# Rewriting the first stage of a hybrid attention layer, up to the first transposed activations

## The chip, the cores and the metric

The kernel runs on one core of a Trainium2 chip. The core has five engines, each with an instruction queue of its own: TensorE (PE, matrix products), VectorE (DVE), ScalarE (ACT), GpSimd (POOL) and SyncE (SP, which here only issues transfers). Each works through its queue in order and waits where an input is not there yet. Transfers between DRAM and the on-chip memory (SBUF) are issued by SP, ACT or POOL and run on 16 DMA engines that all queues share. Products land in PSUM, of which one bank holds 128 x 512 f32.

The metric is the device time of one execution in microseconds (us), as a median of runs.

## The reference

One decoder layer over 2048 rows of 1024. A vector `c` gives a shift, a scale and a gate (adaLN); the rows are normalised, modulated, projected once for two kinds of attention, gated, projected back, normalised and added to the input.

```python
mod = jax.nn.silu(c) @ w_ada[l] + b_ada[l]
shift, scale, gate = jnp.split(mod, 3, axis=-1)
h = rms_norm(x, g_pre[l]) * (1.0 + scale[:, None, :]) + shift[:, None, :]
proj = h @ w_in[l]
qa, ka, va, fa, za, qb, kb, vb, zb = jnp.split(proj, split_points, axis=-1)
oa = forgetting_attention(qa, ka, va, fa + b_fgate[l])      # reshaped to heads
oa = oa * jax.nn.silu(za)
ob = sliding_window_sink_attention(rope(qb), rope(kb), vb, sinks[l])
ob = ob * jax.nn.silu(zb)
y = jnp.concatenate([oa, ob], axis=-1) @ w_out[l]
x = x + gate[:, None, :] * rms_norm(y, g_post[l])
```

What matters here is all that stands before the first product of `h` with a piece of `w_in`: `silu(c) @ w_ada` for shift and scale, the mean squares of the first rows of `x`, the rotary angles, and the preparation of the first weights.

## The kernel before

**Number format.** Large products run on f16 pairs. A f32 matrix is scaled by a power of two and split into a high f16 half and a low one (what is left); a product is then three f16 products (high-high, high-low, low-high). So each piece of weights needs the maximum of its absolute values first, and so does `h`: `pH` is a power of two below a bound on `h`, and `Gp` and `Shp` are gain and shift divided by it.

**h^T.** The 2048 rows are four chunks of 512 (`ci`); `hT[ci]` holds chunk `ci` transposed, for each of eight groups `k` of 128 columns a high and a low tile of 128 x 512. `turn(ci, k)` transposes four 128 x 128 blocks of normalised x on PE into one PSUM tile (five such tiles in rotation); `scaled` then writes the f32 tile `hf` (three in rotation) by ACT with gain and shift, for even `k` the high half too; `split` writes the high half by DVE for odd `k`, and the low half by DVE.

**The first stage** (lines 418 to 642) is written in one block of manual order: within such a block each engine executes in the order of the text. It loads rows, `w_ada` (eight blocks of 512 KB for the scale, `load_ada(1, k)`, eight for the shift, `load_ada(0, k)`), x rows 0 to 3 (`load_x`), the first weights `kb`, `vb`, `zb0` and x rows 4 to 7. `silu(c) @ w_ada` is done on PE with the vector repeated over 128 columns (`ada_pe`, f32 products) and partly on DVE (`ada_dve`: multiply and add into `acc`, summed over partitions by `ada_sum`). `ada_col` takes a result that lies in every partition back to one column per group by a product with the identity and a sum on DVE. `squares`, `root` and `normal` make the mean squares (ACT), their inverse roots (DVE) and the scaled rows. The bound on `h` is 32 times the gain plus the shift, its maximum taken over columns, by a transpose over partitions, and spread again by a product (lines 613 to 621). `spread` sends the rotary factors to their partitions.

**The second block** (from line 1042) runs the projections. Its work on PE is a list `punits` of units; for chunk 0 these are eight of `kb`, eight of `vb`, eight of `zb0`, eight of `zb1`, with `turn_x(1, k)` for the next chunk put in between (`at_`, line 948). Before unit `n` the functions in `events[n]` are written out, and after every second unit `tick` runs what earlier units left for later (evacuations). The two blocks are merged by a planner with estimated times, each block's own order on each engine being kept; so an instruction of the second block can come ahead of later ones of the first.

**A weight's way** (`add`, line 900): eight steps with leads in units ahead of its first product: `w_load` (POOL's queue, 512 KB), `w_max` (maximum per partition on DVE; POOL stores it to DRAM, `mx_d`), `w_back` (POOL loads it back, spread over all partitions, `mxr`), `w_scale` (maximum and power of two on DVE), `w_high` (ACT), `w_low` twice (DVE), `w_done`. For `zb0` maximum and spread are done on chip instead (`z_row` and `z_all`, lines 927 to 934, through PSUM bank 2). `evac_rope` (line 687) evacuates `kb` and `qb`: ACT copies, SP swaps halves by four transfers (`qs`), POOL multiplies by the sine (line 711), DVE adds (line 712), ACT and DVE split.

**The windows.** After `N_PRO - 4` units the sliding-window attention starts: `scores` (PE), `maxima` (DVE), `exps` (ACT), `turn` (PE) per window, with the remaining projection units in between.

## Time and profile before

| what | value |
|---|---|
| median of 3 runs | 1220.69 us (1217.82 to 1222.75) |
| profiled execution, device time | 1218.8 us |
| its span, first to last instruction | 1216.6 us |
| PE busy | 1158.6 us, 95% of the span |
| DVE, ACT, POOL busy | 74%, 55%, 12% |
| mean granted PE clock | 0.985 of full speed |
| moved by DMA | 120.71 MB |

The profile is of one execution. An instruction's row gives its start and length, engine, line of the kernel, operation, `output<-input`, shape, and in brackets the time its engine stood idle before it and what ended that. A row with `xN` merges N neighbours. A transfer's row on SP or POOL is its issue; its landing is seen by who waits for it. In a table of stretches the columns are the stretch, its length, busy time (and count) of PE, PE's weight loads, DVE, ACT and POOL, then the granted PE clock, the share of time the DMA engines were busy, and GB/s; where PE alone is asked for, only PE's column stands between length and clock.

### The profile page before, as it was taken

Reading aid. Unit: us, or ns where it says so; the run is one execution under the profiler, and the core shown is the slowest. Engines: PE = TensorE matmul, PEld = TensorE weight load, DVE = VectorE, ACT = ScalarE, POOL = GpSimd, SP = SyncE. Lnnn points to the kernel's source line nnn. Section 1 sums busy time; section 2 is a strip of 40 time slices with the busy share of each in tenths; the row PEclk is TensorE's granted clock in tenths of the full one; section 3 lists DMA queues with packets and bytes.
Section 4 is the critical chain, followed back from the end, with each engine's and each line's share of the span. In section 5 each row is a group of like instructions: output and inputs, shape, how many; then the busy total and the mean of one; then the engine's idle time right before and its main releaser. Section 6 shows DMA issues by size and latency. Waiting matters only on the chain.

```text
span 1216.6 us, 27400 instructions
## 1 busy us (share of the span) xinstructions
PE 1158.6 (95%) x10832; PEld 693.8 (57%) x10832; DVE 904.4 (74%) x2268; ACT 674.7 (55%) x1117; POOL 142.7 (12%) x252
## 2 busy tenths in 40 slices
PE   6599989999999999999999999999999979999997
PEld 2367657655568876555555555555555545555553
DVE  6676657677777647688888798878978797666665
ACT  2675435555555542566666666666766778333231
POOL 2001122233322211010010110010000000000000
PEclk8899999999999999999999999999999989999999
DMA  9645333334322322323334322122111135445652
GB/s 324 204 131 168 82 77 60 67 94 92 96 78 69 57 60 54 72 61 82 83 60 84 86 60 79 39 71 49 39 44 43 58 117 187 144 156 191 198 169 83
DMA packets 88036, 120.71 MB, mean 99 GB/s; under 512 B 27836, under 2 KB 63716, under 8 KB 87908
## 3 DMA queue, kind: packets, MB, share of 16 engines
q1 hardware_dynamic: 76932, 85.94, 24.3%
q0 software_dynamic: 10976, 33.03, 12.0%
q8 instruction: 85, 1.39, 0.6%
q14 instruction: 43, 0.35, 0.1%
HBM read 71.56 MB, written 25.18 MB: 80 GB/s over the span
## 4 chain that ended last, share of the span: by engine, by line
PE 82%; DVE 9%; DMA 5%; issue 2%; ACT 2%; SPq 1%; POOL 0%; DVEq 0%; ACTq 0%; POOLq 0%
PE bk L307 32%; PE bk L1406 13%; PE bk L325 6%; PE sta L1257 4%; PE bk L1208 4%; PE sta L1258 4%; PE poa L1283 2%; PE poa L1284 2%; PE poa L1281 2%; PE pxb L864 2%; PE bk L740 2%; DMA qs<-qf 2%; PE pss L831 2%; PE pob L883 2%; DVE pha L1271 1%
## 5 line engine op out<-in xcount | busy, mean ns | idle before, releaser
L1264 ACT ACTIVATE p<-sta,lift,scl_qk 128x1024 f32<-128x1024 f32 (+2 forms) x160 | 172.0, 1075 | 135.1 <-PE sta L1258 78.7
L307 PE MATMUL bk<-hT,wh_qk 128*128 128x512 f16 x768 | 194.7, 378 | 0.4 <-DVE a_m L1211 0.4
L1406 PE MATMUL bk<-wohl,oz 128*128 128x512 f16 x768 | 172.4, 379 | 1.9 <-ACT wohl L1346 0.8
L1271 DVE TENSOR_TENSOR pha<-p,pha 128x1024 f16<-128x1024 f32 (+2 forms) x160 | 169.1, 1057 | 0.0
L1211 DVE TENSOR_REDUCE a_m<-bk 128x1 f32<-128x512 f32 x192 | 130.2, 686 | 52.3 <-PE bk L1208 51.7
L1268 ACT ACTIVATE pha<-p 128x1024 f16<-128x1024 f32 (+2 forms) x160 | 148.0, 925 | 6.4 <-PE poa L1284 1.3
L1406 PEld LDWEIGHTS <-oz 128*128 128x128 f16 x768 | 74.4, 99 | 83.9 <-issue 1.8
L1281 PE MATMUL poa<-vt,pha 128*128 128x65 f16 x1088 | 117.4, 193 | 2.7 <-DVE ona L1290 2.7
L1284 PE MATMUL poa<-vt,pha 128*128 128x65 f16 x1088 | 117.1, 193 | 1.1 <-DVE pha L1271 1.1
L1283 PE MATMUL poa<-vt,pha 128*128 128x64 f16 x1088 | 117.4, 195 | 0.0
L1257 PE MATMUL sta<-T 128*128 128x512 f16 (+1 forms) x320 | 112.2, 351 | 4.7 <-ACT p L1264 4.6
L307 PEld LDWEIGHTS <-wh_qk 128*128 128x128 f16 x768 | 72.4, 97 | 75.3 <-issue 1.4
L1208 PE MATMUL bk<-T 66*128 66x512 f16 (+2 forms) x320 | 109.8, 349 | 2.9 <-DMA T<-stq 2.4
L1281 PEld LDWEIGHTS <-pha 128*128 128x128 f16 x1088 | 102.4, 97 | 17.4 <-DVE ona L1290 3.8
L1258 PE MATMUL sta<-T 69*128 69x512 f16 (+1 forms) x320 | 111.1, 352 | 0.0
L1283 PEld LDWEIGHTS <-pha 128*128 128x128 f16 x1088 | 101.5, 97 | 11.5 <-issue 0.3
L1284 PEld LDWEIGHTS <-pha 128*128 128x128 f16 x1088 | 101.5, 99 | 1.3 <-DVE pha L1271 1.3
L307 PE MATMUL bk<-hT,wh_za 128*128 128x512 f16 x384 | 99.8, 378 | 0.0
L325 PE MATMUL bk<-wh_va,hT 128*128 128x128 f16 x1536 | 93.0, 221 | 2.6 <-DVE wh_va L251 2.3
L325 PEld LDWEIGHTS <-hT 128*128 128x128 f16 x1536 | 89.1, 99 | 8.3 <-issue 5.4
L307 PE MATMUL bk<-hT,wh_zb 128*128 128x512 f16 x384 | 89.8, 379 | 0.0
L307 PE MATMUL bk<-hT,wh_qb 128*128 128x512 f16 x384 | 87.4, 379 | 0.0
(491 smaller groups left out, 1872.4 us busy)
## 6 DMA issues: line engine op xcount, KB each, us to landing
wa<-in_w_ada_dram SPq DMA_DIRECT2D x16, 512.0 KB
z_d<-tz POOLq DMA_DIRECT2D x32, 256.0 KB, 2.7
T<-stq SPq DMA_DIRECT2D x128, 64.0 KB
T<-o_d SPq DMA_DIRECT2D x16, 512.0 KB
T<-z_d SPq DMA_DIRECT2D x16, 512.0 KB
xr<-in_x_dram SPq DMA_DIRECT2D x16, 512.0 KB
out_dram<-yg SPq DMA_DIRECT2D x15, 512.0 KB
xt<-in_x_dram SPq DMA_DIRECT2D x12, 512.0 KB
```

Of the source, the lines that this page charges most:

```text
L307: PE.matmul(ps, whl[:, a, k, :], hT[ci][:, b, k, :], start=(k == 0 and n == 0), stop=(k == KT - 1 and n == 2))
L325: PE.matmul(ps[:, u * P:(u + 1) * P], hT[ci][:, a, k, u * P:(u + 1) * P], whl[:, b, k, :], start=(k == 0 and n == 0), stop=(k == KT - 1 an ...
L1208: PE.matmul(mx[:, :w], T[0:XM, 0, i * P:(i + 1) * P], T[0:XM, 2, pc * CH:pc * CH + w], start=True, stop=True)
L1257: PE.matmul(self.st[:, o:o + w], T[:, 3, kb_], T[:, 1, qc], start=True, stop=False)
L1258: PE.matmul(self.st[:, o:o + w], T[0:XR, 2, kb_], T[0:XR, 0, qc], start=False, stop=not diag)
L1264: A.activation(self.p32[:, :self.w], self.st[:, :self.w], AF.Exp, scale=scl[f"qk{self.hd}"][:], bias=lift[:])
L1268: A.activation(self.ph[:, 0, :self.w], self.p32[:, :self.w], AF.Copy)
L1271: V.tensor_tensor(self.ph[:, 1, :self.w], self.p32[:, :self.w], self.ph[:, 0, :self.w], op=ALU.subtract)
L1281: PE.matmul(po[:, u, :], ph[:, 0, pq], vt[:, b, hd, 0:65], start=(self.first and n == 0 and u == 0), stop=False)
L1283: PE.matmul(po[:, u, 0:64], ph[:, 0, pq], vt[:, b, hd, 65:VW], start=False, stop=False)
L1284: PE.matmul(po[:, u, :], ph[:, 1, pq], vt[:, b, hd, 0:65], start=False, stop=(self.last and n == len(self.blocks) - 1))
L1406: PE.matmul(py, self.hl[:, i, k, :], w_slot(8 * j + k)[:, cc], start=(k == 0 and m_ == 0), stop=(k == KT - 1 and m_ == 2))
```

## The change

- **Transfers.** The position and frequency loads go from SP's queue to ACT's, first of all. `zb0` is loaded once, by SP, and no more by POOL at the start. x rows 0 to 3 are loaded ahead of all the shift's `w_ada` blocks.
- **Bound.** `pH` is now taken from a bound that is the sum of two: `pre`, from gain and `b_ada`, reduced over partitions early (`over_all`), and the largest absolute value of the products for the shift, which lie in every partition, so that DVE reduces them on all partitions at once (`rm`) with no transpose.
- **One-column products.** `ada_col` no longer uses the identity: ACT copies one row of a result (`ada_row`), and PE turns it into columns by products with a single one, four for each half.
- **Splits on three engines.** For chunk 0 ACT writes the high half only for `k` = 0; for the others DVE does, and the low halves of `k` = 2, 4, 6 go to POOL.
- **Order.** Scaling and high halves of `kb` and `vb` come earlier; the squares of rows 4 to 7 come between the last tiles of chunk 0; `root(1)` and `normal(1)` move into the second block (events 9 to 13), `z_row` and `z_all` to 8 and 11.
- **Second block.** `zb1`'s steps stand at events 2, 12, 14, 20, 23, 25, 26, 27 (before: 0, 1, 3, 12, 16, 18, 20, 21); the later four leads of `va` and `zb` weights grow by two or three units; chunk 1's turns start three units later; the windows start after `N_PRO - 2` units.

```diff
+        high = k % 2 == 0 if ci else k == 0
...
+            (G if ci == 0 and k in (2, 4, 6) else V).tensor_tensor(lo, hf[:], hi, op=ALU.subtract)
...
+        for g in range(4):
+            A.dma_start(posi[32 * g:32 * g + 32, :], positions[0, g * CH:(g + 1) * CH].partition_broadcast(32))
+        A.dma_start(ifr[:], inv_freq)
...
-        for key in first:
+        for key in first[:2]:
             w_load(key, pieces(key))
...
+        def ada_row(half, n):
+            A.activation(acc[half][0:1, n * CH:(n + 1) * CH], pm[half][n][0:1, :], AF.Copy)
+
+        def ada_col(half, n):
+            for k in range(4 * n, 4 * n + 4):
+                o = 2 * P + 8 * half + k
+                PE.matmul(bk[0][:, o:o + 1], acc[half][0:1, k * P:(k + 1) * P], ones[0:1, 0:1], start=True, stop=True)
...
-        for k in range(3):
-            load_ada(0, k)
         for t in range(4):
             load_x(t)
-        for k in range(3, KT):
+        for k in range(KT):
             load_ada(0, k)
         w_load("zb0", pieces("zb0"), SP)
...
+        def over_all(cols_, dst, name):
+            n = cols_.shape[1]
+            PE.transpose(bk[0][0:n, 0:P], cols_, ident[:])
+            m = st.tile([n, 1], F32, name=f"m{name}")
+            V.tensor_reduce(m[:], bk[0][0:n, 0:P], axis=AX.X, op=ALU.max)
+            d = st.tile([n, n], F32, name=f"d{name}")
+            V.tensor_scalar(d[:], ident[0:n, 0:n], m[:], None, op0=ALU.mult)
+            PE.matmul(bk[0][:, P:P + n], ones[0:n, :], d[:], start=True, stop=True)
+            V.tensor_copy(dst, bk[0][:, P:P + n])
...
+        V.scalar_tensor_tensor(bnd[:], absg[:], 32.0, shb[:], op0=ALU.mult, op1=ALU.add)
+        V.tensor_reduce(mx3[:, 2:3], bnd[:], axis=AX.X, op=ALU.max)
+        pre = st.tile([P, 1], F32, name="pre")
+        ada_dve(0, 1, True)
         ada_pe(0, 0, True)
+        over_all(mx3[:, 2:3], pre[:], "p")
+        V.tensor_scalar(pre[:], pre[:], 1.0e-30, None, op0=ALU.max)
+        w_high("kb")
         root(0)
+        ada_pe(0, 2)
+        ada_dve(0, 3, False)
         normal(0)
+        ada_pe(0, 4)
+        w_low("kb", 0, 1)
+        w_high("vb")
+        ada_dve(0, 5, False)
+        w_low("vb", 0, 1)
+        rm = [st.tile([P, 1], F32, name=f"rm{n}") for n in range(2)]
         for n in range(2):
             nn = slice(n * CH, (n + 1) * CH)
             PE.matmul(pm[0][n][:], ones[:], acc[0][:, nn], start=False, stop=False)
+            for k in (6, 7):
+                PE.matmul(pm[0][n][:], silb[:, k, :], wa[0, k][:, nn], start=False, stop=k == 7)
+                if n and k == 6:
+                    ada_row(0, 0)
+                    ada_col(0, 0)
+            V.tensor_reduce(rm[n][:], pm[0][n][:], axis=AX.X, op=ALU.max, apply_absolute_value=True)
+        ada_row(0, 1)
+        turned = [turn(0, k) for k in range(4)]
+        ada_col(0, 1)
+        turned.append(turn(0, 4))
+        bm = st.tile([P, 1], F32, name="bm")
+        V.scalar_tensor_tensor(bm[:], rm[0][:], rm[1][:], pre[:], op0=ALU.max, op1=ALU.add)
+        V.tensor_scalar(pH[:].bitcast(I32), bm[:].bitcast(I32), 0x7F800000, None, op0=ALU.bitwise_and)
...
         for k in range(KT):
             turned[k][0]()
             turned[k][1]()
-            if k == 2:
-                V.tensor_reduce(mxs[:, 2:3], wq["zb0"][0][:], axis=AX.XY, op=ALU.max, apply_absolute_value=True)
             if k + 5 < KT:
                 turned.append(turn(0, k + 5))
-        root(1)
-        normal(1)
+            if k > 3:
+                squares(1, (k - 4,))
+            if k == 5:
+                V.tensor_reduce(mxs[:, 2:3], wq["zb0"][0][:], axis=AX.XY, op=ALU.max, apply_absolute_value=True)
...
+            leads = (42, 31, 21, 14, 10, 8, 7, 5) if key[:2] in ("va", "zb") else (42, 31, 21, 12, 8, 6, 4, 3)
...
+                elif key == "zb1":
+                    events.setdefault((2, 12, 14, 20, 23, 25, 26, 27)[n], []).append(f)
                 else:
-                    events.setdefault(max(at - lead, n), []).append(f)
+                    events.setdefault(max(at - leads[n], n), []).append(f)
...
-    at_slice(6, z_row)
-    at_slice(10, z_all)
+    at_slice(8, z_row)
+    at_slice(9, lambda: root(1))
+    for u in range(4):
+        at_slice(10 + u, lambda u=u: normal(1, (u,)))
+    at_slice(11, z_all)
...
-            at_ = [14, 16, 18, 20, 22, 24, 26, 28]
+            at_ = [14, 16, 18, 20, 22, 24, 26, 28] if ci else [17, 19, 21, 23, 25, 27, 29, 31]
...
-        fill(N_PRO - 4, tick2)
+        fill(N_PRO - 2, tick2)
...
-        fill(2, tick2)
         for n, wd in enumerate(windows):
```

107 lines of the change are left out of this document (34 added, 73 removed).

## The prediction

> **What bounds the kernel now.** I read the page's slices first (PE is full from the sixth on), then each engine's busy time by stretches, then the timelines of PE, DVE, ACT, SP and POOL up to 90 us, and last what single waits and transfers cost.
>
> ```profile
> 64.00:84.00 20.00, 20.00 (x180) 14.37 (x179) 16.61 (x53) 17.00 (x27) 1.87 (x2) 1.00 0.64 181
> 20.00:22.00 2.00, 2.00 (x6) 0.93 (x5) 1.90 (x4) 0.51 (x1) 0.00 (x0) 0.91 1.04 416
> 22.96 8.20 DMA xt<-in_x_dram
> 50.15 1.22 DVE L211 TENSOR_REDUCE w_mx<-wr_zb 128x1 f32<-128x1024 f32 x1 [4.99 <-DMA wr_zb<-in_w_in_dram]
> 53.90 0.78 ACT L396 ACTIVATE hT<-px,Shp,Gp 128x512 f16<-128x512 f32 x1 [4.74 <-DVE pfl L627]
> 63.71 0.59 PE L307 MATMUL bk<-hT,wh_kb 128*128 128x512 f16 x2 [0.16 <-DVE hT L401]
> ```
>
> The second column of a stretch is its length, the third what PE was busy: 20.00 of 20.00 us in 64 to 84. Before that two moments count. H is 53.90, when ACT writes the first h^T tile; K is 63.71, when the last split of h^T chunk 0 lets PE go for good. The first stage is worth what it moves K. Up to H the transfers run without a pause (DMA share 1.04, 416 GB/s at 20 us; the last of the first four x rows arrives at 31.16), and then DVE stands 4.99 us at a maximum of zb1's weights. That maximum belongs to the later block, but in DVE's order it is ahead of the bound that H needs. So all after K moves with K, unless a new wait comes in.
>
> **The transfers.** The kernel loads zb0 twice, by POOL and by SP; the first copy is dropped, and x0 to x3 go ahead of w_ada(0,0) to (0,2).
>
> ```profile
> wr_zb<-in_w_in_dram SPq DMA_DIRECT2D x1, 512.0 KB
> q0 software_dynamic: 1232, 3.78, 11.2%
> 35.05 1.98 PE L471 MATMUL bk<-wa,silb 128*128 128x512 f32 x4 [0.47 <-DMA wa<-in_w_ada_dram]
> ```
>
> POOL's queue moved 3.78 MB in 11.2% of 130 us, 0.26 MB/us, so the 0.52 MB copy takes 2.0 us; a w_ada block at 0.41 MB/us takes 1.28. The last x row comes 2.0 + 3 x 1.28 = 5.8 us earlier, at 25.4, w_ada(0,1) two blocks later, at 28.0, and w_ada(0,5) at 35.05 - 2.0 = 33.05. The position loads leave SP's queue for ACT's, where their five issues stand ahead of the tanh that w_ada's products need; PE's 3.04 us of waiting for the first w_ada block covers them, and what went beyond it would be paid in full.
>
> ```profile
> 7.05 3.48 PE L471 MATMUL pm<-wa,silb 128*128 128x512 f32 x4 [3.04 <-DMA wa<-in_w_ada_dram]
> 32.43 0.17 DVE L92 TENSOR_SCALAR rs_v<-ss 128x4 f32<-128x4 f32 x1 [0.86 <-ACT junk L372]
> 34.80 4.27 ACT L382 ACTIVATE xt<-xt,rst 128x1024 f32<-128x1024 f32 x4 [2.41 <-DVE rst L106]
> 40.15 1.28 DVE L251 SCALAR_TENSOR_TENSOR wh_kb<-wr_kb,w_sw,wh_kb 128x1024 f16<-128x1024 f32 x1 [0.96 <-ACT wh_kb L245]
> L480 DVE SCALAR_TENSOR_TENSOR acc<-wa,sil,acc x4: 1266/1284/1285, 23.3 to 36.4; 128x1024 f32<-128x1024 f32 x4
> 37.77 1.12 PE L588 MATMUL bk<-acc,ones 128*128 128x512 f32 x2 [0.43 <-DVE acc L480]
> 41.31 2.35 PE L390 MATMUL px<-ident,xt 128*128 128x128 f32 x20
> 51.49 0.37 PE L617 MATMUL bk<-ident,bmx 128*1 128x128 f32 x1 [7.84 <-DVE bmx L615]
> 52.24 0.58 PE L620 MATMUL bk<-bm,ones 1*128 1x1 f32 x2 [0.37 <-DVE bm L619]
> ```
>
> **The chain to H.** DVE's order gives it: w_ada(0,1) at 28.0 and its product, 0.85 (a scaling alone, under the 1.28 of the fused ones); the rest of the early maximum over partitions, 1.4 (as from 51.49 to the end of 52.24 + 0.58, the transpose taken off and two small steps put on); the root of the first rows, 32.43 to 34.80 or 2.35; product (0,3), low half of kb and product (0,5), about 1.25 each: 36.3. Then PE: six products of two records; eight records took 37.77 to 41.31, 0.44 each, so 5.3. The one-column products are not in the trace. Four may cost 0.2 to 1.2 (two records of the nearest, one column wide, 0.58); I take 0.5, since most of the 0.58 is latency that is paid once. That gives 42.1. Sixteen transposes at 0.11 (20 in 2.35) to 43.85, four more columns 0.5, the shift's two small steps 0.4: H at 44.75. The rows maxima on all partitions (0.7, DVE) and ACT's one-row copies (under 0.6) lie beside the transposes; without that cover they cost 0.7. The scalings on ACT (4.27, from 32.6) and vb's high half after them hold DVE's low half of vb until 39.3, still under PE's products. H can lie between 42.5 (if PE waits only for w_ada(0,7), 35.6) and 48.9 (53.90 less the 4.99 us wait alone).
>
> ```profile
> 54.58 1.44 ACT L396 ACTIVATE hf<-px,Shp,Gp 128x512 f32<-128x512 f32 x2
> 84.57 1.06 ACT L372 ACTIVATE junk<-xt 128x1024 bf16<-128x1024 f32 x1
> 85.75 1.06 ACT L372 ACTIVATE junk<-xt 128x1024 bf16<-128x1024 f32 x1
> 59.13 0.41 DVE L400 CAST hT<-hf 128x512 f16<-128x512 f32 x1
> 59.58 1.29 DVE L401 TENSOR_TENSOR hT<-hf,hT 128x512 f16<-128x512 f32 x2
> 69.16 1.28 POOL L711 TENSOR_TENSOR qs<-qs,sinT 128x512 f32<-128x512 f32 x1 [8.29 <-DMA qs<-qf]
> L251 DVE SCALAR_TENSOR_TENSOR wh_zb<-wr_zb,w_sw,wh_zb x8: 739/744/833, 70.2 to 299.3; 128x512 f16<-128x512 f32 x8
> ```
>
> **H to K.** It took 9.81. ACT now makes nine tiles, not twelve (0.66 each, pitch), but three squares of the next rows (1.18 each: 84.57 to 85.75) come before the last tile: 9 x 0.66 + 3 x 1.18 = 9.5; then cast and subtraction, 0.35 + 0.65: 10.55 with the hand-over. Formerly the squares ran under the transfers. Three subtractions go to POOL, 1.28 each by the row of its only like operation. One DVE instruction with two inputs in SBUF lay partly under that POOL row; it took 0.83 where its fellows take 0.74. Three full collisions of about 0.5 would be 1.5; none is 0; by that small row I take 0.5. K comes at 55.85, 7.85 earlier.
>
> The Trainium skill, SBUF — State Buffer, section Who interferes with whom, says that a DVE instruction with two SBUF inputs and a GpSimd one that reads SBUF shut each other out for a whole instruction. The trace has only the 0.83; by the page the sum would be about 1 us higher.
>
> **After K: the weights of zb1.** This is the part against the change. The maximum moves to event 12 of the second block, its read-back to 14, scaling to 20, and zb1's first product is unit 28. The maximum goes through DRAM: DVE, POOL's store, POOL's load, DVE.
>
> ```profile
> DMA to landing us min/median/max: 8.1/8.3/9.8
> DMA to landing us min/median/max: 4.4/5.0/6.7
> 51.67 0.56 POOL L214 DMA_DIRECT2D mx_d<-w_mx  x1 [9.02 <-DVE bmx L615]
> 60.33 0.54 POOL L219 DMA_DIRECT2D mxr<-mx_d  x1 [8.11 <-DMA mx_d<-w_mx]
> 140.24 0.29 DVE L230 TENSOR_REDUCE w_mx<-mxr 128x1 f32<-128x128 f32 x1 [5.10 <-DMA mxr<-mx_d]
> 141.34 0.69 DVE L702 SCALAR_TENSOR_TENSOR qc<-bk,cosT 128x512 f32<-128x512 f32 x1
> 66.57 1.41 DVE L384 TENSOR_SCALAR hT<-hT,rst 128x1024 f32<-128x1024 f32 x2
> 141.32 1.15 ACT L245 ACTIVATE wh_qb<-wr_qb,w_sw 128x1024 f16<-128x1024 f32 x1 [1.81 <-DVE w_sw L237]
> 76.95 1.46 PE L307 MATMUL bk<-hT,wh_zb 128*128 128x512 f16 x6
> ```
>
> The first two rows are L214's store and L219's load, over 23 keys; the pair takes 13.3. At 60.33 that wait lay under the first stage. Now DVE reaches the maximum late: from K on two products of kb and zb0's row maximum (0.43, then 0.7 as from 51.49 to 52.24: 1.1), the root of the next rows, moved here (2.35), the cosine product (0.6), two scalings (1.3 of the pair's 1.41), zb0's copy (0.1) and scale (0.75: 140.24 to 141.34 without the reduction), the maximum itself (1.2, as at 50.15): K + 7.4. POOL issues at + 7.7, loads at + 16.0, it lands at + 21.0; scaling 1.05 (140.24 to 141.3); ACT's high half 1.15: K + 23.3. Behind that load on POOL stands the sine product, DVE's next step waits for it, and then DVE stands at the scaling. So the low half comes after three overdue DVE steps (2.25) and lasts 0.74: K + 25.15. PE wants it at K + 13.9 (zb1 now starts one unit, 0.65, after 76.95, which is K + 13.9; a turn of 0.44 fewer ahead of it, two products of 0.43 more before the low half). The stall is 11.3; it contains 2.1 on the way, where PE waits for a bank that zb0's copy reads behind the root (1.4) and for zb0's low half (0.7). Bounds: with minima 9.6, with maxima 14.7.
>
> ```profile
> 56.00:57.00 1.00, 1.00 (x7) 0.50 0.00 0
> 58.00:59.00 1.00, 1.00 (x8) 1.00 0.00 0
> ```
>
> An idle PE also loses its clock (third number from the right): still 0.50 in 56 to 57, two us after work restarted, 1.00 from 58. Restarting at 0.50 for some 3.2 us loses 1.6 (0 to 2.5). The split of chunk 1, which now starts three units later, would else delay PE by 1.3; both fall together.
>
> **Leads and first scores.**
>
> ```profile
> 164.47 0.28 PE L831 MATMUL pss<-kst,stb 64*128 64x128 f16 x4 [1.34 <-ACT stb L713]
> 177.59 6.92 PE L325 MATMUL bk<-wh_va,hT 128*128 128x128 f16 x94 [2.33 <-DVE wh_va L251]
> 170.51 0.29 DVE L230 TENSOR_REDUCE w_mx<-mxr 128x1 f32<-128x128 f32 x1 [2.83 <-DMA mxr<-mx_d]
> 173.46 0.82 PE L864 MATMUL pxb<-ident,sm__1912 128*128 128x128 f32 x6
> ```
>
> Two more units ahead of the first scores cover the 1.34; va0's low half two units earlier removes the 2.33. But va0's scaling now stands ahead of the first window's maxima on DVE and waits for the same load, 170.51, so its exponentials come some 5 us later and the transposes of 173.46 about 2, the 1.34 counted. Together -0.3 (-3.5 to +2).
>
> **Sum.** -7.85 + 11.3 + 1.6 - 0.3 = +4.75 on the profiled execution's 1218.8 (span 1216.6), which is 1.9 under the median, 1220.69. On the median: 1225.4. A measurement of this kernel can tell about 0.5%, 6.1 us, from no change; 4.75 is less.
>
> **Rivals.** *The round trip is hidden (0.20).* If the pair takes under 5.5 us, or DVE reaches the maximum early, as it did at 50.15, only the 2.1 remains: -7.85 + 2.1 - 0.3 = -6.05, 1214.6. Against it: no store of the 23 landed under 8.1, and the maximum now stands behind zb0's row maximum, which waits for PE.
>
> The Trainium skill, DMA: Bandwidth & Descriptors, section Anatomy of one DMA, gives about 2.0 us of fixed cost for each transfer on this path; by that the pair would take 4 and this rival would hold. The rows, 8.3 and 5.0, contradict it.
>
> *The first stage gains only the removed wait (0.16), the slower one.* Place: DVE's strict order ahead of the six products, where the scaling of the rows on ACT, vb's high half and DVE's low half follow one another. If x arrives as late as now, or PE's products end after 46, H is 48.9: K gains 3.7, the sum is -3.7 + 11.3 + 1.6 - 0.3 = +8.9, 1229.6. It decides from H at about 46.5, where the sum passes 6.1. For it: transfers are full to 44 us in the table of stretches. Against it: fewer bytes ahead of x.
>
> *The parts cancel (0.06):* the change does not do what it says; what K gains the new waits return, 1220.7.
>
> The forecast itself has 0.58. Its low ends together (H at 42.5, minima, no loss of clock, -3.5) give -4.0; its high ends (full collisions, maxima, 2.5, +2) give +12.3; not all fall together, so its own range is 1218.5 to 1231. Slower by over 0.5% takes 0.20 of its chance and 0.12 of the second rival's: 0.32. Faster takes 0.11 of the first rival's, which lies on the bound, and 0.01 elsewhere: 0.12. The rest is 0.56. The whole range is 1213.5 to 1231.
>
> **What would show it.** Right: the fourth x load landing near 25.4; H near 45 and no DVE wait for wr_zb before it; K near 56; PE's longest wait at zb1's first product, released by DVE or ACT writing wh_zb, about 8 us, with the store and load rows before it; clock 0.50 behind it. Wrong: no wait of over 3 us between K and K + 20, or H after 47.

## The result, and the profile after

The changed kernel takes 1233.57 us (median of 5 runs, 1229.22 to 1236.34) where the kernel before, run beside it, takes 1220.69 (5 runs, 1217.82 to 1223.14). The ratio is 1.0104 with a 95% interval of 1.0083 to 1.0126: 12.9 us slower. The forecast was 1225.4 and the range ended at 1231.0, so the sign was right and the size was not: the forecast had given being slower by over 0.5% a chance of 0.32, and no chance to a time above 1231.

Two more marks are used from here on, because they can be read in every kernel's profile: V, when PE starts the first product of vb (0.4 us behind K), and C, when it starts chunk 1's first product of kb. The timeline of PE in the kernel before has them at 64.14 and 84.09.

```profile
64.14 1.58 PE L740 MATMUL bk<-wh_vb,hT 128*128 128x136 f16 x24
84.09 1.24 PE L307 MATMUL bk<-hT,wh_kb 128*128 128x512 f16 x5
```

Rows from the timeline of the changed kernel up to H, all engines together, sorted by start:

```profile
27.31 1.91 PE L491 MATMUL bk<-ones,acc 1*128 1x1 f32 x16 [0.34 <-DVE mxs L575]
27.55 1.06 ACT L372 ACTIVATE junk<-xt 128x1024 bf16<-128x1024 f32 x1
29.15 3.52 PE L470 MATMUL bk<-wa,silb 128*128 128x512 f32 x4
30.22 0.74 DVE L477 TENSOR_SCALAR acc<-wa,sil 128x1024 f32<-128x1024 f32 x1
32.92 0.28 DVE L571 TENSOR_REDUCE mp<-bk 1x1 f32<-1x128 f32 x1 [1.95 <-PE bk L569]
34.17 0.16 DVE L92 TENSOR_SCALAR rs_v<-ss 128x4 f32<-128x4 f32 x1
36.54 4.27 ACT L382 ACTIVATE xt<-xt,rst 128x1024 f32<-128x1024 f32 x4 [6.81 <-DVE rst L106]
40.15 2.08 PE L612 MATMUL bk<-acc,ones 128*128 128x512 f32 x2 [2.65 <-DVE acc L479]
45.21 0.59 ACT L486 ACTIVATE acc<-bk 1x512 f32<-1x512 f32 x1 [3.31 <-DVE rm L618]
46.09 1.05 PE L491 MATMUL bk<-ones,acc 1*128 1x1 f32 x8
48.96 0.59 ACT L486 ACTIVATE acc<-bk 1x512 f32<-1x512 f32 x1 [3.16 <-DVE rm L618]
49.87 1.05 PE L491 MATMUL bk<-ones,acc 1*128 1x1 f32 x8
51.48 0.78 ACT L398 ACTIVATE hT<-px,Shp,Gp 128x512 f16<-128x512 f32 x1 [1.94 <-DVE shf L632]
```

The fourth x row is there by 27.55 (its square starts without a wait), so the transfers did what was forecast. H is 51.48 and not 44.75. DVE comes to its product of w_ada(0,1) at 30.22, without a wait, where the forecast had 28.0: small steps of its own, for the gain and the bound, stand ahead of it, and these wait for PE's one-column products (the row at 27.31). Then comes the early maximum over partitions. It lasts until 34.17, for DVE waits 1.95 us for a product of PE that stands behind the row at 29.15, and that row shows four records in 3.52 us, twice the 0.44 each of the sum. Behind the maximum stands the root (34.17), behind that the scaling of the rows (36.54, ACT idle for 6.81) and DVE's last product, for which PE waits 2.65 us. The table of stretches gives the reason for the 3.52 (columns: stretch, length, busy PE, weight loads, DVE, ACT, POOL, granted clock, DMA share, GB/s):

```profile
30.00:31.00 1.00, 1.00 (x3) 0.48 (x2) 0.93 (x3) 0.00 (x0) 0.00 (x0) 0.50 1.03 410
40.00:41.00 1.00, 0.85 (x1) 0.50 (x2) 0.10 (x1) 1.00 (x2) 0.11 (x1) 0.50 1.01 401
```

PE's granted clock is 0.50 in both. In the profile of the kernel before it is 1.00 from 26 to 46 us.

From H to C in the changed kernel's timeline:

```profile
60.94 1.32 POOL L403 TENSOR_TENSOR hT<-hf,hT 128x512 f16<-128x512 f32 x1 [2.09 <-DVE hT L402]
61.28 1.52 DVE L403 TENSOR_TENSOR hT<-hf,hT 128x512 f16<-128x512 f32 x1
62.31 1.24 PE L307 MATMUL bk<-hT,wh_kb 128*128 128x512 f16 x5 [1.02 <-POOL hT L403]
63.49 2.29 PE L746 MATMUL bk<-wh_vb,hT 128*128 128x136 f16 x36
67.73 3.00 PE L746 MATMUL bk<-wh_vb,hT 128*128 128x136 f16 x48 [0.82 <-DVE mxs L941]
68.90 1.21 DVE L211 TENSOR_REDUCE w_mx<-wr_zb 128x1 f32<-128x1024 f32 x1
70.40 0.57 POOL L214 DMA_DIRECT2D mx_d<-w_mx  x1 [8.15 <-DVE w_mx L211]
78.82 0.54 POOL L219 DMA_DIRECT2D mxr<-mx_d  x1 [7.84 <-DMA cosT<-cs__240]
84.57 0.29 DVE L230 TENSOR_REDUCE w_mx<-mxr 128x1 f32<-128x128 f32 x1 [2.66 <-DMA mxr<-mx_d]
86.86 1.03 PE L307 MATMUL bk<-hT,wh_zb 128*128 128x512 f16 x2 [8.83 <-ACT wh_zb L245]
88.61 1.89 PE L307 MATMUL bk<-hT,wh_zb 128*128 128x512 f16 x4 [0.71 <-DVE wh_zb L251]
97.90 2.32 PE L307 MATMUL bk<-hT,wh_kb 128*128 128x512 f16 x10
```

DVE's last split, which took the wait's place at K, ends at 61.28 + 1.52 = 62.80, and V is 63.49: the whole first stage gained 0.65 us. Then comes the way through DRAM: the store issued at 70.40, the load at 78.82 (its row names cosT as what ended the wait, so it doesn't tell when the store had landed), PE waiting 8.83 and 0.71 us for zb1's two halves. From V to C it takes 34.41 us, formerly 19.95: 14.5 lost. C is 13.8 us late. (The two profiled executions differ by 1235.95 - 1218.8 = 17.15 us; the other 3.3 come behind C, but 4.3 is where the two lie against their medians, 2.4 above and 1.9 below, so nothing can be read from them.)

```profile
82.00:86.00 4.00, 0.00 (x0) 0.00 (x0) 1.29 (x6) 2.38 (x5) 0.00 (x0) 0.50 0.78 291
90.00:94.00 4.00, 4.00 (x14) 2.17 (x13) 2.62 (x5) 4.00 (x7) 0.59 (x1) 0.50 0.25 81
```

PE is idle in 82 to 86 and still at half clock in 90 to 94, when it is busy all the time.

### The profile page after: what moved, and what is told of

Read it like the earlier page. It is cut to its first block, busy times and chain, and to the rows that moved or that the text cites. A ratio compares the mean times of both kernels' runs of the same rounds, so it can differ in the third digit from the quotient of the medians.

```text
span 1234.3 us, 27468 instructions
## 1 busy us (share of the span) xinstructions
PE 1175.4 (95%) x10868; PEld 700.7 (57%) x10868; DVE 905.0 (73%) x2266; ACT 674.1 (55%) x1118; POOL 144.2 (12%) x254
## 3 DMA queue, kind: packets, MB, share of 16 engines
q0 software_dynamic: 10832, 32.50, 11.3%
## 4 chain that ended last, share of the span: by engine, by line
PE 76%; DVE 11%; DMA 6%; issue 3%; ACT 2%; SPq 1%; POOL 1%; DVEq 0%; POOLq 0%; ACTq 0%
PE bk L307 28%; PE bk L1416 12%; PE bk L325 5%; PE sta L1267 4%; PE bk L1218 4%; PE sta L1268 4%; PE poa L1293 2%; PE poa L1291 2%; PE poa L1294 2%; DMA qs<-qf 2%; PE pxb L870 2%; PE pob L889 1%; PE pss L837 1%; DVE pha L1281 1%; DVE a_m L1221 1%
## 5 line engine op out<-in xcount | busy, mean ns | idle before, releaser
L307 PE MATMUL bk<-hT,wh_qk 128*128 128x512 f16 x768 | 197.7, 383 | 0.4 <-DVE a_m L1221 0.4
L307 PE MATMUL bk<-hT,wh_zb 128*128 128x512 f16 x384 | 92.8, 388 | 9.7 <-ACT wh_zb L245 8.8
```

Of the source, the lines that this page charges most:

```text
L307: PE.matmul(ps, whl[:, a, k, :], hT[ci][:, b, k, :], start=(k == 0 and n == 0), stop=(k == KT - 1 and n == 2))
```

## The experiments

Ratios are to the kernel before, run on the same chip beside each kernel; that kernel's median was 1213.91 to 1214.54 us in these sets. H, V and C are read from each kernel's own timeline. The marks of the kernel before come from the first set, whose median was 1220.69; E5, whose first stage is as before, has them within 0.3 us of these in a set of 1214, so they may be compared.

| | kernel | ratio, 95% interval | H | V | C |
|---|---|---|---|---|---|
| | before | 1 | 53.90 | 64.14 | 84.09 |
| | changed | 1.0104 (1.0083 to 1.0126) | 51.48 | 63.49 | 97.90 |
| E1 | changed, zb1's steps back | 1.0032 (1.0015 to 1.0049) | 52.23 | 64.75 | 85.93 |
| E2 | before, zb1's steps late | 1.0060 (1.0040 to 1.0080) | 48.70 | 58.92 | 91.32 |
| E3 | changed, zb1's maximum on chip | 1.0156 (1.0122 to 1.0189) | 51.12 | 63.75 | 85.94 |
| E4 | changed, root first | 1.0081 (1.0054 to 1.0107) | 49.54 | 61.55 | 96.44 |
| E5 | before, second block's part | 1.0001 (0.9988 to 1.0014) | 53.61 | 64.39 | 84.35 |
| E6 | changed, DVE's sum last | 1.0091 (1.0072 to 1.0111) | 48.51 | 60.53 | 92.49 |
| E7 | changed, no split on POOL | 1.0104 (1.0076 to 1.0132) | 48.99 | 60.39 | 93.25 |
| E8 | E3, E4, E6 together | 1.0149 (1.0127 to 1.0171) | 48.93 | 61.55 | 84.30 |
| E9 | changed, PE kept busy | 1.0142 (1.0125 to 1.0160) | 54.26 | 66.28 | 101.16 |
| E10 | E8, small tiles elsewhere | 1.0144 (1.0116 to 1.0172) | 49.89 | 62.51 | 85.26 |
| E11 | before, zb1's maximum on chip | 1.0043 (1.0028 to 1.0059) | 48.68 | 59.67 | 80.08 |
| E12 | changed, again | 1.0105 (1.0089 to 1.0121) | 50.91 | 62.93 | 97.79 |
| E13 | E11 and an unread store and load | 0.9960 (0.9945 to 0.9975) | 48.64 | 59.64 | 80.04 |
| E14 | E10 and an unread store and load | 1.0010 (0.9996 to 1.0025) | 47.08 | 59.70 | 83.95 |
| E15 | E11 and two small loads | 1.0062 (1.0040 to 1.0084) | 49.31 | 60.31 | 80.71 |
| E16 | E11, one buffer passed over | 1.0062 (1.0040 to 1.0085) | 48.48 | 59.48 | 79.88 |
| E17 | E11 and the pair, other buffers | 0.9973 (0.9958 to 0.9988) | 48.20 | 59.18 | 79.58 |
| E18 | E13 with another order | 0.9977 (0.9963 to 0.9991) | 48.29 | 59.27 | 79.68 |

### E1 and E2: zb1's steps alone, taken out and put in

```diff
 E1, in the changed kernel
-    events.setdefault((2, 12, 14, 20, 23, 25, 26, 27)[n], []).append(f)
+    events.setdefault((0, 1, 3, 12, 16, 18, 20, 21)[n], []).append(f)
 E2, in the kernel before
+                elif key == "zb1":
+                    events.setdefault((2, 12, 14, 20, 23, 25, 26, 27)[n], []).append(f)
```

> The changed kernel with zb1's eight steps put back to their former events (0, 1, 3, 12, 16, 18, 20, 21); all else of the change stays. Theory T (the change loses its time behind K, in zb1's maximum that goes to DRAM and back while PE waits for zb1's weights: waits of 8.83 and 0.71 us at its first products and about 3 us of half clock behind them): the maximum comes back ahead of H, where DVE may again wait up to 5 us for zb1's weights; PE's wait at zb1's first product falls from 8.8 to under 1 us, the clock stays at 1.00 there, chunk 1's first product of kb comes at 84 to 88 instead of 97.9, and the time is 1219 to 1226 us. Rival R (the time is lost in the first stage itself or in the leads of the second block): within 4 us of 1233.6.

> The kernel before with one part of the change alone: zb1's steps at events 2, 12, 14, 20, 23, 25, 26, 27. Theory T: DVE's wait of 4.99 us ahead of H goes, K comes 3 to 5 us earlier (59 to 61), but store (about 8.3) and load (about 5.0) now stand between K and zb1's first product, which waits 8 to 10 us with the clock at 0.50 behind it: 1226 to 1232 us. Rival R (the late maximum is covered, the loss lies elsewhere): only the removed wait shows, 1215 to 1218 us.

E1's timeline:

```profile
46.99 1.22 DVE L211 TENSOR_REDUCE w_mx<-wr_zb 128x1 f32<-128x1024 f32 x1 [0.89 <-DMA wr_zb<-in_w_in_dram]
85.93 4.70 PE L307 MATMUL bk<-hT,wh_kb 128*128 128x512 f16 x21
```

The maximum is ahead of H again, and DVE now waits 0.89 us there, not 4.99, since zb1's weights arrive earlier. PE has no wait at zb1's first product; C is 85.93 instead of 97.90, and the ratio falls from 1.0104 to 1.0032: about 8.8 us of the 12.9. E2's timeline:

```profile
48.70 0.76 ACT L396 ACTIVATE hT<-px,Shp,Gp 128x512 f16<-128x512 f32 x1
58.92 1.58 PE L740 MATMUL bk<-wh_vb,hT 128*128 128x136 f16 x24
80.81 1.03 PE L307 MATMUL bk<-hT,wh_zb 128*128 128x512 f16 x2 [8.27 <-ACT wh_zb L245]
91.32 5.34 PE L307 MATMUL bk<-hT,wh_kb 128*128 128x512 f16 x24
```

One part alone has both effects: V comes 5.2 us earlier, C 7.2 later, in all 0.6% (7.3 us) slower, in the lower half of what the theory gave, and far from its rival. Both runs put the loss behind K on zb1's way through DRAM. E2 shows a second thing: the kernel before, with nothing done but its wait removed, has H at 48.70 and V at 58.92. That is earlier than the rewritten stage's 51.48 and 63.49. So what zb1's way does not explain is the rewriting itself.

### E5: the second block's part

```diff
 in the kernel before (zb1 keeps its leads)
+            leads = (42, 31, 21, 14, 10, 8, 7, 5) if key[:2] in ("va", "zb") and key != "zb1" else (42, 31, 21, 12, 8, 6, 4, 3)
-        fill(N_PRO - 4, tick2)
+        fill(N_PRO - 2, tick2)
```

> The kernel before with the part of the second block alone: the longer leads for va and zb keys (zb1 and the first stage untouched) and two more units ahead of the first scores. In the runs so far the stretch from va0's first product to the fox stage's first product is 2.5 to 6.6 us shorter with this part (before: 174.97 to 441.59, 266.6 us; zb1 put back to its former events: 177.00 to 436.97, 260.0 us). Theory L (this part is worth 4 to 6 us, not the 0.3 of the prediction): 4 to 6 us faster than the kernel before, its waits of 1.34 and 2.33 us at first scores and va0 gone. Rival (as predicted, or the stretch varies by itself): within 1.5 us of the kernel before.

1.0001. The two waits are gone and the stretch is 261.6 us in this profile (174.19 to 435.82), not 266.6, but the time is the same within 0.14%. The profile of the kernel before is of a slower set (median 1220.69), and that of E5 is the second lowest of its ten runs, so the shorter stretch is no effect that can be told from the runs' spread. The interval, some 1.6 us to either side, holds the forecast's -0.3 and does not measure it. E5 leaves out chunk 1's later turns and the moved root and scaling.

### E4, E6, E7, E9, E12: what holds H back

```diff
 E4
         ada_pe(0, 0, True)
+        root(0)
         over_all(mx3[:, 2:3], pre[:], "p")
...
-        root(0)
 E6
...
+            if n == 0:
+                ada_pe(0, 6)
+                ada_pe(0, 7)
-            PE.matmul(pm[0][n][:], ones[:], acc[0][:, nn], start=False, stop=False)
-            for k in (6, 7):
-                PE.matmul(pm[0][n][:], silb[:, k, :], wa[0, k][:, nn], start=False, stop=k == 7)
+            PE.matmul(pm[0][n][:], ones[:], acc[0][:, nn], start=False, stop=True)
 E7
-            (G if ci == 0 and k in (2, 4, 6) else V).tensor_tensor(lo, hf[:], hi, op=ALU.subtract)
+            V.tensor_tensor(lo, hf[:], hi, op=ALU.subtract)
 E9: twelve of these in PE's gaps
+                PE.matmul(dm[:], silb[:, 0, :], silb[:, 0:4, :].rearrange("p k n -> p (k n)"), start=True, stop=True)
```

> The changed kernel with one reordering on DVE: the root of the first rows stands ahead of the early maximum over partitions, which waits for PE. Theory T' (H is late because DVE, in its order, waits for a PE that runs at half clock): root ends at about 31.5 instead of 36.5, DVE's last product (0,5) about 1.2 us earlier, H at 49.5 to 50.5 instead of 51.48, time 1 to 2 us lower, 1231.5 to 1232.5, which 3 rounds may not tell. Rival (PE's own work and the rows' scaling set H): H unmoved within 0.3 us.

> The changed kernel with PE's last six products in another order: w_ada(0,6) and (0,7) first, the two products with the sum that DVE gathers last. Theory C (PE waits 2.65 us for DVE's product (0,5) and then starts at half clock, so H is late by PE's order, not by DVE's or ACT's work): PE works on from 37.5 with no wait of over 1 us and at clock 1.00 to the end of the products, which end at 43.5 to 45 instead of 48.03; H at 47 to 48.5 instead of 51.48, all behind it 3 to 4 us earlier, time 3 to 4 us lower than the changed kernel's 1.0104 of before (1.007 to 1.008). Rival (DVE's or ACT's own work sets H): H within 1 us of 51.48, 1.010.

> The changed kernel with the three subtractions that it gives to POOL in the first stage back on DVE. Theory (DVE and POOL shut each other out: DVE's three subtractions beside POOL's take 1.52 instead of 0.69, and POOL hands over the last but one 1.25 to 1.42 after it starts): DVE takes 3 x 0.65 more of its own and saves 3 x 0.83, so from H to K about 10.3 instead of 11.3, K at 61.8; time lower by up to 1 us (1.009 to 1.0104 of before). Rival (POOL's help is needed): from H to K 12 or more, time higher by about 1 us.

> The changed kernel with products that nobody reads put into PE's gaps of the first stage, so that PE's clock does not fall: one behind each transpose of an early maximum (0.44 us each), two behind each four one-column products of the first half, six ahead of the sum that DVE gathers (the gap there was 2.65 us). Theory C' (the half clock in 29 to 32.5 and 40 to 43 costs H 3 to 4 us): granted clock 1.00 from 28 to 50, the product of w_ada(0,0) 1.9 us instead of 3.52, the last six products with their columns 6.8 to 7 instead of 7.9 us, H 1.5 to 3 us earlier than in the changed kernel on the same chip. Rival (the clock costs little, or the fillers take back what it gives): H within 1 us, time within 0.2%.

> The changed kernel itself once more, on the chip of these runs, as the base for the others: 1.008 to 1.013 of the kernel before; H between 49 and 52, chunk 1's first product of kb between 93 and 98 (other kernels with the same first stage showed H near 49.5 on other chips, the changed one 51.48).

The changed kernel again (E12) gives 1.0105, so the result stands in another set of runs, with the kernel before at 1213.91. But H in the profiles that have the same chain up to H is 51.48, 50.91 (E12), 51.12 (E3), 52.23 (E1, with 1.2 us of maximum in it) and 48.99 (E7, whose edit begins behind H): it moves by 2.5 us, and so does the stretch at half clock (29.46 to 32.87 and 39.70 to 43.11 in the changed kernel, 28.54 to 38.78 in E12, 30.27 to 37.09 in E7). So H of E4 (49.54) and of E6 (48.51) does not settle what they bring, and their times do not either (intervals that overlap the changed kernel's). PE's wait of 2.65 is gone in E6, as expected. What can be told is the two together with ACT's row copies put ahead of DVE's row maxima, below (E14).

E9 speaks on the clock. The table of stretches of E12 first, then of E9, and PE's timeline of one and the same product, E12's row first:

```profile
30.00:38.00 8.00, 7.39 (x11) 2.89 (x11) 4.59 (x24) 0.57 (x1) 0.00 (x0) 0.50 1.06 381
```

```profile
28.00:38.00 10.00, 10.00 (x31) 4.81 (x31) 4.10 (x24) 1.31 (x3) 0.00 (x0) 1.00 1.05 387
```

```profile
29.57 3.78 PE L470 MATMUL bk<-wa,silb 128*128 128x512 f32 x4
32.71 1.88 PE L470 MATMUL bk<-wa,silb 128*128 128x512 f32 x4
```

With unread products in its gaps PE keeps the full clock; without them it stays at 0.50 for eight us in which it is 92% busy. The same product takes 1.88 us instead of 3.78. The twelve fillers are 24 records of 0.43, 10.4 us of work, and H comes only 3.35 us later than in E12. Still later, so both sides were wrong: the half clock is a real cost, and filling does not pay. From the first product of the early maximum to the last of the six products, PE's own work takes 13.2 us in E12 (15.4 less 2.2 idle) and about 8.8 in E9 (19.2 less the fillers' 10.4). So the half clock costs about 4.4 us of PE's time there; the fillers cost more than that and the idle time together.

The Trainium skill, TensorE: Matmul & The Clock Gate, section Part 1, says that one busy window of some 3.4 us gives the full clock back. The length agrees: at half clock the changed kernel, E12 and E7 spend 3.41 us twice, 10.24 and 6.83 us, whole multiples of 3.41. Which window counts as busy can't be read from the profile's busy share. The table of stretches of E12, then of E14, each for one such window:

```profile
28.54:31.95 3.41, 3.41 (x9) 2.19 (x9) 1.57 (x7) 1.15 (x3) 0.00 (x0) 0.50 1.04 413
```

```profile
31.03:34.45 3.42, 2.81 (x5) 0.64 (x4) 2.88 (x16) 0.60 (x1) 0.00 (x0) 0.50 1.03 398
```

E12's is full, its first 1.0 us with one-column products, and the clock stays at 0.50 behind it; E14's is busy for 2.81 us, and the clock is back at its end. A window of E6 with 2.80 busy (29.46 to 32.87) did not bring it back.

E7 settles the collisions. The timeline of its DVE has the low halves at the one length, where the changed kernel has three of 1.52 or 1.53 beside POOL:

```profile
55.85 0.69 DVE L403 TENSOR_TENSOR hT<-hf,hT 128x512 f16<-128x512 f32 x1
```

From H to V it takes 11.40 in E7, 12.01 in the changed kernel, 10.24 before. So POOL's help costs 0.6 us instead of bringing any, as the theory had it, and the time does not show it (1.0104). The 1.2 us that are left between E7 and the kernel before were not taken apart: the squares put ahead of the last tiles lie there, and so do the casts moved to DVE.

### E3, E8, E10, E11: zb1's maximum on the chip

```diff
+        V.tensor_reduce(mxs[:, 3:4], wq["zb1"][0][:], axis=AX.XY, op=ALU.max, apply_absolute_value=True)
...
-        PE.transpose(bk[2][0:1, 0:P], mxs[:, 2:3], ident[:])
+        PE.transpose(bk[2][0:2, 0:P], mxs[:, 2:4], ident[:])
...
-        PE.matmul(bk[2][:, P:P + 1], ones[0:1, :], mz[:], start=True, stop=True)
+        PE.matmul(bk[2][:, P:P + 2], ones[0:2, :], dz[:], start=True, stop=True)
 E3 loads zb1's weights by POOL's queue, E8, E10 and E11 by SP's
 E8 adds E4 and E6, copies zb0's scale earlier, puts the second columns behind two turns, and ACT's row copies ahead of DVE's row maxima:
+            ada_row(0, n)
             V.tensor_reduce(rm[n][:], pm[0][n][:], axis=AX.X, op=ALU.max, apply_absolute_value=True)
-        ada_row(0, 1)
 E10 is E8 with mxs[:, 2:4], mz and dz in one tile of the pool trig
 E11 is the kernel before with the same, and
-        for key in first:
+        for key in first[:2]:
             w_load(key, pieces(key))
```

> The changed kernel, but zb1's weights are loaded in the first stage as soon as kb's buffer is free, and their maximum is taken over the partitions together with zb0's, by one transpose and one product on the chip, with no store to DRAM and no load. The other steps of zb1 stay at their events. Theory T: the wait at zb1's first product falls under 1 us, no half clock behind it, chunk 1's first product of kb at 84 to 87; H and K as in the changed kernel (51.5 and 62.8), or up to 1.5 later for the maximum's 1.2 us on DVE: 1217 to 1223 us. Rival R: 1229 us or more.

> The changed kernel with what the runs so far point to, together: zb1's maximum on the chip with zb0's (its weights by SP's queue behind the x rows), the root ahead of the early maximum, the two products with DVE's sum last, ACT's row copies ahead of DVE's row maxima, zb0's scale copied ahead of the second root. Theory: H at 45 to 47, K at 56 to 58.5, no wait over 1 us at zb1's first product, chunk 1's first product of kb at 79 to 82 (before 84.09, changed 97.90): 0.991 to 0.996 of the kernel before. Rival Q (the loss behind 437 us that the run with zb1's maximum on the chip showed, 9.4 us for T's row and 8 us of issue time, belongs to this arrangement): 1.002 to 1.010 of before though chunk 1 starts early.

> The combined kernel of the run before, with its three new small tiles taken from the free end of a pool that closes early, instead of from the constants in front of all other tiles. Same instructions, same order; every later tile lies where it lies in the changed kernel (they were shifted by 32 bytes a partition). Theory Q (the shift, not zb1's maximum on the chip, made T's rows late at 458 and PE stand for want of instructions behind it): chunk 1 at 84 to 85 as before, no issue wait over 1 us behind 480, the last part from T's first products to the end 755 to 758 us instead of 769: 0.998 to 1.003 of the kernel before. Rival (the late loss comes from the order or the timing of the second block): 1.012 to 1.017 again.

> The kernel before with two edits and nothing of the change's first stage: zb1's weights are loaded behind the x rows and their maximum taken on the chip together with zb0's, behind the last split; zb0 is loaded once. Theory (what was to be had was the 4.99 us wait ahead of H, without a way through DRAM behind K): H at 48 to 50 instead of 53.90, K at 58.5 to 61 instead of 63.71, no wait over 1 us at zb1's first product, chunk 1 at 79.5 to 82 instead of 84.09: 0.996 to 0.998 of the kernel before. Rival (the wait only moves: to PE's z row, or to zb0's scale): chunk 1 within 1 us of 84.09, same time.

E3 and E11 start chunk 1 as early as expected (85.94 and 80.08), E10 just behind (85.26), E8 not (84.30, its H at 48.93). All four are slower than their starts allow: E11 gains 4 us at C and ends 0.43% behind. The loss lies far behind, where nothing was edited. POOL's timeline of E11 in the fox stage, and the lines on the loads' landing and on PE's waits behind 440 us:

```profile
561.74 0.56 POOL L216 DMA_DIRECT2D mx_d<-w_mx  x1 [18.87 <-DVE w_mx L213]
562.86 0.54 POOL L216 DMA_DIRECT2D mx_d<-w_mx  x1 [0.57 <-DVE w_mx L213]
569.17 0.54 POOL L221 DMA_DIRECT2D mxr<-mx_d  x1 [5.76 <-DMA mx_d<-w_mx]
578.67 0.54 POOL L221 DMA_DIRECT2D mxr<-mx_d  x1 [8.96 <-DMA mx_d<-w_mx]
```

```profile
DMA to landing us min/median/max: 3.2/4.4/13.9
```

```profile
PE bk L1215 <- DMA T<-rw: 5.1, 1, 5.1
PE poa L1288 <- issue: 2.6, 1, 2.6
PE poa L1290 <- issue: 0.9, 1, 0.9
```

Two weights follow each other here, each with a store and a load. The second load can go only at 578.67, 15.8 us after its store; a load takes up to 13.9 us (the profile knows the landing of 11 of E11's 22); PE waits 5.1 us for a row of T and 3.5 us for nothing that the profile shows. In the kernel before no load took over 6.7 us, but landing is known there for 5 of 23 only, and PE waits 2.4 us for the same row. E10 has the small tiles where they shift nothing, and the loss is the same: the placing theory falls.

### E13 to E18: what gives it back

```diff
 E13 (in E11) and E14 (in E10); zb1's weights go by POOL's queue again
+        G.dma_start(mx_d[0][:], mxs[:, 0:1])
+        mxr0 = mxp.tile([P, P], F32, tag="mxr", name="mxr")
+        G.dma_start(mxr0[:], mx_d[0][:].rearrange("p o -> (p o)").partition_broadcast(P))
 E15: instead of the pair
+        for _ in range(2):
+            G.dma_start(snk[:], sinks[0].partition_broadcast(P))
 E16: instead of the pair
+        mxp.tile([P, P], F32, tag="mxr", name="mxr")
 E17: the pair, but
+        G.dma_start(zero[:, 0:P], mx_d[0][:].rearrange("p o -> (p o)").partition_broadcast(P))
 E18 (in E13): transpose and product of kb's and vb's maximum ahead of ada_pe(0, 3);
 w_high("kb") ahead of normal(0), w_high("vb") ahead of squares(1), w_low("kb") behind ada_dve(0, 6)
```

> The kernel before with zb1's maximum on the chip, as in the run of that kind (chunk 1 at 80.08, but 1.0043 of before), with three things put back: zb1's weights by POOL's queue, and a store of 128 x 4 bytes to DRAM with its load into 128 partitions, which nobody reads, in the first stage. POOL's queue so counts the transfers that it counts in the changed kernel. Theory S (the loss behind 440 us comes with the place of later transfers in POOL's queue, which moves when transfers ahead of them are left out): store and load of the later pairs land as in the kernel before (the second load of a pair under 3 us behind the first, no load over 7 us), no issue wait over 1 us behind 480, chunk 1 at 79.5 to 81.5, 0.995 to 0.998 of the kernel before. Rival (the loss comes from the on-chip maximum or from the earlier time itself): 1.003 to 1.006 again.

> The combined kernel (chunk 1 at 84.3 to 85.3, but 1.0149 and 1.0144 of before) with the same three things put back. Theory S: the last part from T's first products to the end 755 to 758 us instead of 769 to 772: 0.998 to 1.002 of the kernel before. Rival: 1.012 to 1.017.

> The kernel before with zb1's maximum on the chip, without the unread store and load, but with zb1's weights by POOL's queue and two more small loads (sinks, 4 KB each, the same data twice more) in it: the number of transfers in POOL's queue is the changed kernel's. Theory S by number alone: 0.995 to 0.998 of before as with the pair. If the kind counts (a store to DRAM and a broadcast load among them): 1.003 to 1.006.

> The kernel before with zb1's maximum on the chip and its weights by POOL's queue; of the unread pair only this is left: one of the three buffers that the loads of maxima take in turn is passed over, so that each later load goes into the buffer that it goes into in the kernel before. No transfer is added. Theory B (the buffer a load goes into decides how long the later pairs take): 0.995 to 0.998 of the kernel before, no load of a maximum over 7 us, no issue wait over 1 us behind 480. Rival (the transfers themselves count, the place in the queue behind a store and a broadcast load): 1.003 to 1.007, loads up to 11 to 14 us.

> The other half: the unread store and its load are made, but into a tile of the first stage that is free by then, so that the later loads' buffers are one place off as in the run without the pair. Theory B: 1.003 to 1.007 of the kernel before, loads up to 11 to 14 us. Rival (the transfers themselves count): 0.995 to 0.998.

> The kernel before with zb1's maximum on the chip and the pair (0.996 of before in its first run), and the early maximum of kb and vb ahead of PE's wait for w_ada(0,3), so that kb's high half lies in ACT's gap ahead of the rows' scaling, and vb's high half ahead of the second rows' squares. Theory: DVE's two products come ahead of kb's low half, H at 46.8 to 47.5 instead of 48.64, chunk 1 at 78 to 79 instead of 80.04: 0.994 to 0.9965. Rival (PE's products, which end at 42.81, set H with DVE's diagonal behind them): H within 0.5 of 48.64, 0.995 to 0.9975.

With a store of 512 bytes and a load that nobody reads, E11 goes from 1.0043 to 0.9960 and E10 from 1.0144 to 1.0010. In both, zb1's weights go by POOL's queue again too; E16 and E13 differ in nothing but the pair, 1.0062 against 0.9960, 12 us. POOL's timeline of E13 at the same place, and its line on landing:

```profile
558.59 0.56 POOL L216 DMA_DIRECT2D mx_d<-w_mx  x1 [18.87 <-DVE w_mx L213]
559.72 0.55 POOL L216 DMA_DIRECT2D mx_d<-w_mx  x1 [0.57 <-DVE w_mx L213]
567.06 0.54 POOL L221 DMA_DIRECT2D mxr<-mx_d  x1 [6.79 <-DMA mx_d<-w_mx]
568.32 0.54 POOL L221 DMA_DIRECT2D mxr<-mx_d  x1 [0.72 <-DMA mx_d<-w_mx]
```

```profile
DMA to landing us min/median/max: 3.4/4.9/5.8
```

The second load now goes 1.3 us behind the first. PE reaches its first product of q and k at 438.7 us in E11, 1.3 ahead of E13, and at 586 us it is 9.3 behind. The same holds wherever, behind 440 us, two weights follow each other, four places in each kernel: the second load goes 5.8 to 9.8 us behind the first in the six kernels without an early pair for zb1 (E3, E8, E10, E11, E15, E16) and 0.5 to 2.9 in the fourteen that make one, read or unread. The transfers themselves take longer. The lines on queues for 20 us from the first of two such stores (packets, MB, share of the engines' time), E11's first, then E13's:

```profile
q0 software_dynamic: 128, 0.13, 20.2%
```

```profile
q0 software_dynamic: 128, 0.13, 7.8%
```

The same 128 packets and bytes take 20.2% in E11 and 7.8% in E13. The buffer that the loads take is not the cause (E16, which turns only that, stays at 1.0062; E17, which leaves it turned and makes the transfers, is at 0.9973): theory B falls. The mere number of transfers in POOL's queue is not it either (E15, whose two small loads stand at the queue's start and not in the pair's place). Left is that a store to DRAM and its broadcast load stand in the queue ahead of the later ones; the store alone, the load alone and their place were not tried. How that works on the later pairs stays open.

E13 beats both kernels: 0.9960 (0.9945 to 0.9975); the medians of all runs of the set, 1210.88 us against 1214.48 for the kernel before, give 0.9970, inside that interval. E18 was to bring H to 47; its H is 48.29, for ACT comes to the first tile only behind the squares of rows 4 to 7, whose transfers land late; it is no better than E13.

E14 is the rewritten stage at its best here, with its waits mended and no way through DRAM: 1.0010 against E13's 0.9960. Its H is 1.6 us earlier than E13's, but V is the same (12.6 us from H, not 11.0), and from V to C it takes 24.25 instead of 20.40, for PE waits 2.37 us for zb0's high half. That stands on ACT but waits for zb0's scale, which DVE ends at 67.09 only: on DVE it comes behind the root and the scalings (61.00 to 66.46) that the change moved there. Half clock follows the wait (0.57 in 68 to 72). What the stage wins ahead of H it gives back behind.

## Why the prediction was wrong, point by point

**Transfers.** Right: x is on time, and DVE's wait of 4.99 us for zb1's weights is gone.

**The chain to H.** This step failed: 44.75 forecast, 51.48 measured. Six of the 6.7 us are two terms. PE's products started at 40.15 and not at 36.3 (3.85). Of that, 2.2 is DVE's queue: the forecast started the chain when w_ada(0,1) arrives, 28.0, and put what stands ahead of its product on DVE (the steps for gain and bound, and their wait for PE's columns) at nothing, without a reason; DVE came to it at 30.22. Another 1.8 is the early maximum, 3.2 us instead of 1.4, queued on PE behind a product at half clock. Root and products came out 0.2 shorter than forecast. Then PE's six products took, with their four columns, 7.9 us instead of 5.8 (2.1), about 1.5 of it half clock and 0.5 the columns. I priced all of PE's f32 records at 0.44 from rows taken at full clock. The rest is small: four one-column products took 1.05 and not 0.5, the second time as well, and ACT's copies of a row did not lie beside DVE's maxima of the same bank but behind them (45.21 and 48.96, ended by DVE). So some 3.2 us are half clock, 2.2 the queue ahead and 1.0 the columns. This split is read from the one profile; E9 shows that the price of the half clock is real, and no run takes out one of the three alone.

**H to K.** Right in sum: 11.3 against 11.05. ACT's nine tiles and three squares ran from 51.48 to 60.78, 9.3 us for 9.5 forecast. The collisions with POOL took more than their full size, 0.83 each and 2.5 in all where 0.5 was taken and 1.5 called full: three subtractions of 1.52 to 1.53 instead of 0.69, as the Trainium skill has it (SBUF — State Buffer, Who interferes with whom); E7, without them, is 0.6 us shorter from H to V. The sum came right, in part by luck, because two of the three lay under ACT's work and only the last on the chain. So K's term, -7.85, came out at -0.9.

**zb1's way through DRAM.** Right: the maximum ended 7.3 us behind K (7.4 forecast), the high half 24.0 (23.3), PE waited 8.83 us (about 8). From V to C 14.5 us were lost where 11.3 and 1.6 for the clock were forecast. The waits make 10.55 (8.83, 0.71 and two of 0.82 and 0.19). The clock stayed at half until about 94, with PE busy for 6.4 of the 7.1 us from 86.86, which loses 3.2 to 3.4 and not 1.6. Some 0.7 stay open. The price of store and load, 13.3, was read as over 23 keys; the trace knows the landing of three stores and five loads only, and the 8.1 is no floor: E2's store landed in 7.5. It fitted here all the same (70.40 to 84.57). E1 takes this term out and recovers 8.8 us of the median.

**Leads.** Not settled: -0.3 forecast, 1.0001 measured, give or take 0.0013 (E5).

**The sum.** -0.9 instead of -7.85 and 14.5 instead of 12.9 make, with the -0.3, +13.3 against 12.9 measured. The second rival (first stage gains only the removed wait, decided from H at 46.5) named the right side and the right place, DVE's order ahead of the six products, and its condition held (PE's products ended at 48.03, after 46). Its mechanism, the scaling on ACT and the two halves one behind the other, was not what set H, and it put the gain at 3.7 from the wait alone, where V gained 0.65. E2 shows that the wait alone is worth 5.2 at V, so the rewriting as such lost 4.6 us there. No case in the forecast had the new chain worse than the old one without its wait. By my own list of signs, H after 47 was the one that said wrong.

## What to carry to other kernels

A wait ahead of a critical chain should first be removed by itself and timed: here that alone was worth more at V than the rewriting (5.2 us against 0.65). A maximum taken on the chip removes the wait with no way through DRAM, but here it made the kernel faster only with the unread pair in the queue (0.9960 with it, 1.0043 without). Before work is moved behind a mark, add up store, load and both engines' queues up to its first user. Start a chain not at the arrival of its data but where the engine's own order lets it begin. And price PE's f32 products at half clock wherever the new order leaves it gaps ahead of them.

## What the runs showed of the hardware that was not expected

PE's clock, once at half, does not come back with the next 3.41 us of work in every case: E12's window of 3.41 busy us of 3.41 left it at 0.50, and E14's of 2.81 brought it back. What makes a window count was not found.

And without an early store and load for zb1 in POOL's queue, later pairs went slowly: with two weights behind each other, the second load went 5.8 to 9.8 us behind the first in the six kernels that leave them out, and 0.5 to 2.9 in the fourteen that make them, among them E13, E14, E17 and E18, where nobody reads them. The slowest load took 10.9 to 13.9 us in the six, and 6.7 at most in the others, among those whose landing is known; not every load was slow (medians 4.4 to 5.9 against 3.6 to 5.0). By E16 against E13 the pair was worth 12 us of the whole; E11 against E17 gives 8.5, and E10 against E14 16 with the weights' queue changed too. What in the queue it depends on was not found.
